# Where the operands of the dense matmuls begin in SBUF: multiples of 64 bytes in place of multiples of 16

## The chip, the cores and the metric

One core of a Trainium2 chip runs one program. The metric is the device time of one execution in microseconds. Three executions of the kernel before gave 1210.40, 1216.53 and 1216.72 us, a median of 1216.53 us.

## What is computed

Two blocks run one after the other on 256 tokens of width 1024, all in float32. The first is a Mamba-2 and RG-LRU hybrid with a gated feed-forward; the second has two layers, each with three mixers (retention, top-k attention, dilated attention) and an MLP of width 4096. Cut to the dense products, which are nearly all of the work:

```
proj = rmsnorm(x) @ w_in                        # 1024 -> 9760
h    = x + (g_ssm*(y_ssm @ w_out_ssm) + g_lru*(y_lru @ w_out_lru)) @ w_out
h    = h + (silu(gate) * up) @ w_ffn_out        # gate, up = split(rmsnorm(h) @ w_ffn_in), 1024 -> 2*2816
for layer in 0, 1:
    x = x + concat(retention, dsa, dilated)(rms_norm(x) @ w_in_2[layer]) @ w_out_2[layer]
    x = x + square(relu(rms_norm(x) @ w_up_2[layer])) @ w_down_2[layer]     # 1024 -> 4096 -> 1024
return rms_norm(x)
```

## The kernel before

Every dense product is done in a split form. A float32 operand is held as a pair of tiles, `hi` (rounded to the matmul's F32R format by ScalarE) and `lo` (the rest, by VectorE), and a product is three matmuls: hi by hi, hi by lo, lo by hi (`mm3`, L329, and L380 to L382).

The weights stream from HBM on the SP queue into three raw buffers (`emit_dma`, L222). `emit_split` (L240) turns a piece of 1024 columns into `hi` (L253, ScalarE) and `lo` (L254, VectorE), four pieces ahead of their use, in five buffers each of 4,096 bytes a partition. `run_a` (L334) uses a 128x128 slice of the weights as the stationary operand (loaded by a weight load ahead of each matmul) and 256 columns of activations as the moving one. `run_b` (L360) does it the other way round: 128 tokens of the activations are stationary, and up to 512 columns of weights move. Small side tasks (convolutions, scans, attention, norms) are cut into steps that `tick` (L285) puts between groups of the dense matmuls, in an order fixed when the program is built.

The activations that are dense operands lie in these tiles: `xn` (the normalised input of a stage, one pair of 8 x 256 columns, reused by six stages in turn; `xn_tiles`, L406, with offsets from `XOFF`, L56); `uh`, `ul`, `sTh`, `sTl`, `lTh`, `lTl` and `mx0`, `mx1` (parts of the first block's mixers, pool `p1`); `ah`, `al` (feed-forward, L980); `mxh`, `mxl` (mixers of the second block, L877); `mah`, `mal` (MLP of each layer, L1297). An element takes 4 bytes, a row of 256 columns 1,024 bytes, and the 128-wide weight slices are 512 bytes apart, so that within a stage all operands of one kind begin at the same place modulo 512.

The starts that the allocator gives, in bytes modulo 512, and the number of dense matmuls that the loops issue:

```
stage (activation tile)           matmuls            activations  weights  moving minus stationary
in (xn 1)                         1848 of 256 cols   288          288      0
lg, wl, ws, wo (uh, lT, sT, mx)   876 of 256         480          288      192
ffn in (xn 3)                     1056 of 256        256          288      480
ffn out (ah)                      528 of 256         448          288      160
mixers 0 (xn 5), run_a            384 of 256         384          288      96
mixers 0 (xn 5), run_b            144 of 512         384          288      416
mixer outputs (mxh 6, mxh 11)     192 of 256, twice  32           288      256
up 0 (xn 8)                       768 of 256         480          288      192
down 0 (mah 0)                    768 of 256         480          288      192
mixers 1 (xn 10), run_a           384 of 256         32           288      256
mixers 1 (xn 10), run_b           144 of 512         32           288      256
up 1 (xn 13)                      768 of 256         304          288      16
down 1 (mah 1), run_b             288 of 512, 192 of 256   448    288      352
```

Modulo 64 the weights begin at 32, and so do the activations at 288, 480 and 32; those at 256, 384 and 448 begin at 0, and those at 304 at 48. One unit of each mixer stage (`kw`, 72 columns) has slices at other places.

Of the kernel before, what the change touches and what calls it, by code (L numbers as in the profile page):

```python
# [10 lines left out]
F32 = mybir.dt.float32  # L11
F32R = mybir.dt.float32r
# [5 lines left out]
T = 256  # L18
# [33 lines left out]
FM, QM, UM = (2, 3), (0, 0), (2, 3)  # L52

XOFF = ((8, 24), (0, 16), (32, 48), (56, 72), (72, 88), (12, 28))  # L56


CT = {"ident": 0, "tri": 128, "dup": 512}
# [63 lines left out]
def _build(ctx, tc, nc, A, out):  # L123
    cp = ctx.enter_context(tc.tile_pool(name="cp", bufs=1))
# [191 lines left out]
    def tpb():  # L316
        return bank("tp", 1)
# [85 lines left out]
    xn_n = [0]  # L403
    xn_s = [0]

    def xn_tiles():  # L406

        offs = XOFF[xn_s[0]]
        xn_s[0] += 1
        xn_n[0] += 1  # L410
        ab = []
        for k, o in zip("hl", offs):
            t = cp.tile([128, 8 * T + 112], F32R, tag=f"xn{k}", name=f"xn{k}{xn_n[0]}")
            ab.append(t[:, o:o + 8 * T].rearrange("p (k t) -> p k t", t=T))
        return ab

    def opnd(pair):
        return lambda k: (pair[0][:, k, :], pair[1][:, k, :])
# [66 lines left out]
    def split_into(hi, lo, src):  # L485
        S.activation(hi, src, AF.Copy)
        V.tensor_sub(lo, src, hi.bitcast(F32))  # L487
# [3 lines left out]
    with ExitStack() as st0:  # L491
# [30 lines left out]
        xn = xn_tiles()  # L522
# [11 lines left out]
        for f in range(0, 8, 2):  # L534
            t = p0.tile([128, 2, T], F32, tag="nx", bufs=2, name=f"nx{f}")
# [9 lines left out]
    p1x = ExitStack()  # L545
    ac = p1x.enter_context(tc.tile_pool(name="ac", bufs=1, side="right", reuse_waits="tile"))
    acs = ac.tile([128, 8, T], F32, name="acs")
    acl = ac.tile([128, 8, T], F32, name="acl")
    p1c = ExitStack()
    p1 = p1c.enter_context(tc.tile_pool(name="p1", bufs=1, side="right", reuse_waits="tile"))  # L550
    X = opnd(xn)
# [192 lines left out]
    ut, hl, lo_t = {}, {}, {}  # L744
# [131 lines left out]

    def mix_tiles(pool):  # L877
        xn_n[0] += 1
        return (pool.tile([128, 8, T], F32R, name=f"mxh{xn_n[0]}"), pool.tile([128, 8, T], F32R, name=f"mxl{xn_n[0]}"))

    class Norm:

# [78 lines left out]
    def rbb(rb, n):  # L961
        return rb[:, None, :].to_broadcast([128, n, T])
# [14 lines left out]

    with ExitStack() as st:
        pf = st.enter_context(tc.tile_pool(name="pf", bufs=1, side="right", reuse_waits="tile"))
        ah = pf.tile([128, 22, T], F32R, name="ah")  # L980
        al = pf.tile([128, 22, T], F32R, name="al")
        X = opnd(nrm.xn)
        for i, (a, b) in enumerate(FT):
            bg = run_a(f"fg{i}", X, hook=nrm.hook(FM) if i == 0 else None)
            sg = []
            for c, ps in enumerate(bg):
                t = pf.tile([128, 2, T], F32, tag="sg", bufs=4, name=f"fsg{i}{c}")
                V.tensor_mul(t, ps.rearrange("p (a b) -> p a b", b=T), rbb(nrm.rb, 2))
                S.activation(t, t, AF.Silu)
                sg.append(t)  # L990
            bu = run_a(f"fu{i}", X)
            for c, ps in enumerate(bu):
                t = pf.tile([128, 2, T], F32, tag="su", bufs=2, name=f"fsu{i}{c}")
                V.tensor_mul(t, ps.rearrange("p (a b) -> p a b", b=T), rbb(nrm.rb, 2))
                V.tensor_mul(t, t, sg[c])
                k = a + 2 * c
                split_into(ah[:, k:k + 2, :], al[:, k:k + 2, :], t)
        wfa = pf.tile([128, 8], F32, name="wfa")
        V.tensor_mul(wfa, pv[:, PV["normf"]:PV["normf"] + 8], pv[:, PV["attn"]:PV["attn"] + 8])
        wfac = cp.tile([128, 8], F32, name="wfac")  # L1000
        V.tensor_copy(wfac, wfa)
        nrm = Norm(lambda t: wfac[:, t:t + 1], second=lambda t: pvc("normf", t))
        for n in range(2):
            banks = run_a(f"fo{n}", opnd((ah, al)))
            for i, ps in enumerate(banks):
                nrm.bank_done(ps, 4 * n + 2 * i)
# [287 lines left out]
    def mlp(l, nrm):  # L1294
        with ExitStack() as st:
            pf = st.enter_context(tc.tile_pool(name=f"pf{l}", bufs=1, side="right", reuse_waits="tile"))
            ah = pf.tile([128, 32, T], F32R, name=f"mah{l}")  # L1297
            al = pf.tile([128, 32, T], F32R, name=f"mal{l}")
            X = opnd(nrm.xn)
            last = l == 1  # L1300
            if last:
                xr = pf.tile([128, 2, D], F32, name="xr")
                fw = pf.tile([128, D], F32, name="fw")
                brow(fw, 608, 608 + D, nc.gpsimd)

                def resid_t():
                    for b in range(2):
                        for c in range(2):
                            ps = tpb()
                            for t in range(4):  # L1310
                                PE.transpose(ps[:, t * 128:t * 128 + 128], h[:, 4 * c + t, b * 128:b * 128 + 128], ident)
                            S.activation(xr[:, b, c * 512:c * 512 + 512], ps, AF.Copy)
                            yield from pause("resid_t1", 1)

            for i in range(8):
                bu = run_a(f"up{i}_{l}", X, hook=nrm.hook(UM) if i == 0 else None)
                if last and i == 0:
                    side.append(resid_t())
                for c, ps in enumerate(bu):
                    k = 4 * i + 2 * c  # L1320
                    t = pf.tile([128, 2, T], F32, tag="mt", bufs=2, name=f"mt{l}{i}{c}")
                    a = pf.tile([128, 2, T], F32, tag="ma", bufs=2, name=f"ma{l}{i}{c}")
                    V.scalar_tensor_tensor(t, ps.rearrange("p (a b) -> p a b", b=T), 0.0, rbb(nrm.rb, 2),
                                           op0=OP.max, op1=OP.mult)
                    S.activation(a, t, AF.Square)
                    split_into(ah[:, k:k + 2, :], al[:, k:k + 2, :], a)
            drain()
            if not last:
                nrm2 = Norm(lambda t: pvc("attn", 8 + t), act=True)
                for n in range(2):  # L1330
                    banks = run_a(f"dn{n}_{l}", opnd((ah, al)))
                    for i, ps in enumerate(banks):
                        nrm2.bank_done(ps, 4 * n + 2 * i)
                return nrm2
            ssf = pf.tile([128, 2, 3], F32, name="ssf")
            for n in range(2):
                if n:
                    warm = sm.tile([128, 1], F32, name="warm")
                    S.activation(warm, ssf[:, 1, 0:1], AF.Sqrt)
                banks = run_b(f"dn{n}_{l}", opnd((ah, al)), tail=3 if n else 1, halves=n == 1)  # L1340
                for b in range(2):
                    parts = ((0, 0, 512), (1, 0, 512)) if n == 0 else ((0, 0, 512), (1, 0, 256), (2, 256, 256))
                    parts = parts[b:1 + b * len(parts)]
                    for i, (k, c0, w) in enumerate(parts):
                        if n and i + 1 == len(parts):
                            part = sm.tile([128, 1], F32, tag="part", name=f"part{b}")
                            V.tensor_scalar(part, ssf[:, b, 0:1], 1.0 / D, EPS, op0=OP.mult, op1=OP.add)
                            if i:
                                V.scalar_tensor_tensor(part, ssf[:, b, 1:2], 1.0 / D, part, op0=OP.mult, op1=OP.add)
                        d = xr[:, b, 512 * n + c0:512 * n + c0 + w]  # L1350
                        V.tensor_add(d, d, banks[k][:, 0:w])
                        q = pf.tile([128, 512], F32, tag="fq", bufs=2, name=f"fq{n}{b}{i}")
                        S.activation(q[:, 0:w], d, AF.Square, accum_out=ssf[:, b, n + i:n + i + 1])
                    if n:
                        r = rsqrt_act(ssf[:, b, len(parts):len(parts) + 1], 1.0 / D, part, f"rf{b}")
                    if n == 0:
                        V.tensor_mul(xr[:, b, 0:512], xr[:, b, 0:512], fw[:, 0:512])
                    else:
                        d0, d1 = xr[:, b, 0:512], xr[:, b, 512:1024]
                        S.activation(d0, d0, AF.Identity, scale=r)  # L1360
                        nc.sync.dma_start(out[0, 128 * b:128 * b + 128, 0:512], d0)
                        V.scalar_tensor_tensor(d1, d1, r, fw[:, 512:1024], op0=OP.mult, op1=OP.mult)
                        nc.sync.dma_start(out[0, 128 * b:128 * b + 128, 512:1024], d1)
# [39 lines left out]
```

## Time and profile before

| | |
|---|---|
| median of three executions | 1216.53 us |
| the profiled execution, its own time | 1216.44 us |
| its span, from the first to the last instruction | 1214.7 us |
| matmuls busy | 1202.6 us, 99% |
| weight loads busy | 1133.3 us, 93% |
| VectorE busy | 846.8 us, 70% |
| ScalarE busy | 700.5 us, 58% |
| the costliest group of matmuls (L330 on `xn`) | 1736 of them, mean record 284 ns |

Matmuls are pipelined: the record of one lasts some 280 ns, and the next begins long before it ends. What counts is the distance from one start to the next, here called the spacing. A stretch of the trace that is full of matmuls gives it as its length over the number that begin in it.

### The profile page before, as it was taken

What the parts mean: (1) busy time and instruction counts of PE and PEld (TensorE: products, weight loads), DVE (VectorE), ACT (ScalarE), POOL (GpSimd) and SP (SyncE); (2) the same over time, 40 slices, a digit from 0 to 9 for tenths busy, and PEclk for the clock granted to TensorE, in tenths of its full rate; (3) what the DMA queues carried; (4) which work ended last, traced back from release to release, by engine and by line L of the source; (5) the groups of instructions that cost most, each with busy time, mean ns of one, the idle gap of its engine ahead of it and who ended that gap; (6) DMA issues with size and microseconds to landing.
All of it is one profiled execution on the core that took longest, in us unless ns stands there. A gap on an engine that the chain in (4) does not pass through costs nothing.

```text
span 1214.7 us, 22653 instructions
## 1 busy us (share of the span) xinstructions
PE 1202.6 (99%) x9369; PEld 1133.3 (93%) x9369; DVE 846.8 (70%) x1483; ACT 700.5 (58%) x1071; POOL 4.6 (0%) x12
## 2 busy tenths in 40 slices
PE   8999999999999999999999999999999999999997
PEld 8999999999999999999897899999997969999886
DVE  7888988987686666557967586655479586666453
ACT  7698788767466444444546575544355376655342
POOL 0000000000000000000000000000000000000000
PEclk9999999999999999999999999999999999999999
DMA  8455444656555655545353455555554434565550
GB/s 299 135 176 172 151 145 150 206 175 204 196 177 177 197 182 178 185 159 194 121 178 105 138 175 179 196 182 183 169 163 143 134 105 158 185 194 175 192 189 35
DMA packets 109382, 205.21 MB, mean 169 GB/s; under 512 B 5792, under 2 KB 15776, under 8 KB 109152
## 3 DMA queue, kind: packets, MB, share of 16 engines
q1 hardware_dynamic: 108560, 201.09, 50.9%
q0 software_dynamic: 576, 2.62, 0.6%
q8 instruction: 73, 1.20, 0.4%
q14 instruction: 29, 0.24, 0.1%
q10 hardware_dynamic: 144, 0.07, 0.0%
HBM read 202.71 MB, written 1.05 MB: 168 GB/s over the span
## 4 chain that ended last, share of the span: by engine, by line
PE 94%; DVE 4%; ACT 1%; DMA 0%; issue 0%; SPq 0%; ACTq 0%
PE ps_mm L330 25%; PE ps_mm L332 25%; PE ps_mm L331 25%; PE ps_mm L380 3%; PE ps_mm L382 3%; PE ps_mm L381 3%; PE ps_sc L327 2%; PE ps_o L1123 1%; PE ps_o L688 1%; DVE lo L254 1%; DVE acc L1069 1%; PE ps_tp L1110 1%; DVE m L1068 1%; PE ps_sc L669 1%; PE ps_tp L941 0%; DMA xt<-in_x 0%
## 5 line engine op out<-in xcount | busy, mean ns | idle before, releaser
L254 DVE TENSOR_TENSOR lo<-raw,hi 128x1024 fp32r<-128x1024 f32 (+2 forms) x382 | 461.9, 1213 | 284.5 <-ACT hi L253 281.4
L253 ACT ACTIVATE hi<-raw 128x1024 fp32r<-128x1024 f32 (+2 forms) x382 | 400.6, 1053 | 425.9 <-PE ps_mm L331 332.5
L330 PE MATMUL ps_mm<-xnh,hi 128*128 128x256 f32 x1736 | 492.4, 284 | 0.0
L331 PE MATMUL ps_mm<-xnl,hi 128*128 128x256 f32 x1736 | 490.3, 283 | 0.0
L332 PE MATMUL ps_mm<-xnh,lo 128*128 128x256 f32 (+1 forms) x1736 | 489.2, 282 | 0.0
L330 PEld LDWEIGHTS ps_mm<-xnh,hi 128*128 128x128 f32 x1736 | 327.9, 189 | 3.8 <-issue 2.5
L331 PEld LDWEIGHTS ps_mm<-xnl,hi 128*128 128x128 f32 x1736 | 329.2, 190 | 1.3 <-DVE xnl L487 0.2
L332 PEld LDWEIGHTS ps_mm<-xnh,lo 128*128 128x128 f32 (+1 forms) x1736 | 328.2, 189 | 0.4 <-issue 0.2
L330 PE MATMUL ps_mm<-mah,hi 128*128 128x256 f32 x256 | 71.9, 281 | 0.0
L331 PE MATMUL ps_mm<-mal,hi 128*128 128x256 f32 x256 | 71.9, 281 | 0.0
L332 PE MATMUL ps_mm<-mah,lo 128*128 128x256 f32 x256 | 71.9, 281 | 0.0
L382 PE MATMUL ps_mm<-hi,mal 128*128 128x256 f32 (+1 forms) x160 | 56.2, 351 | 0.0
L381 PE MATMUL ps_mm<-lo,mah 128*128 128x256 f32 (+1 forms) x160 | 55.9, 349 | 0.0
L380 PE MATMUL ps_mm<-hi,mah 128*128 128x256 f32 (+1 forms) x160 | 55.7, 348 | 0.0
L330 PE MATMUL ps_mm<-ah,hi 128*128 128x256 f32 x176 | 49.2, 280 | 0.0
L331 PE MATMUL ps_mm<-al,hi 128*128 128x256 f32 x176 | 49.2, 280 | 0.0
L332 PE MATMUL ps_mm<-ah,lo 128*128 128x256 f32 x176 | 49.2, 280 | 0.0
L331 PEld LDWEIGHTS ps_mm<-mal,hi 128*128 128x128 f32 x256 | 49.2, 192 | 0.0
L330 PEld LDWEIGHTS ps_mm<-mah,hi 128*128 128x128 f32 x256 | 48.1, 188 | 0.0
L332 PEld LDWEIGHTS ps_mm<-mah,lo 128*128 128x128 f32 x256 | 48.1, 188 | 0.0
L380 PE MATMUL ps_mm<-hi,xnh 128*128 128x512 f32 x96 | 39.1, 407 | 0.0
L382 PE MATMUL ps_mm<-hi,xnl 128*128 128x512 f32 x96 | 37.8, 394 | 0.0
(384 smaller groups left out, 1885.1 us busy)
## 6 DMA issues: line engine op xcount, KB each, us to landing
raw<-in_w_in SPq DMA_DIRECT2D x61, 1024.0 KB, 5.1
raw<-in_w_up SPq DMA_DIRECT2D x32, 1024.0 KB, 5.4
raw<-in_w_down SPq DMA_DIRECT2D x32, 1024.0 KB, 5.0
raw<-in_w_ffn_in SPq DMA_DIRECT2D x22, 1024.0 KB, 5.2
raw<-in_w_ffn_out SPq DMA_DIRECT2D x10, 1024.0 KB, 5.1
raw<-in_w_out_ssm SPq DMA_DIRECT2D x8, 1024.0 KB, 5.1
raw<-in_w_out SPq DMA_DIRECT2D x16, 512.0 KB, 3.8
raw<-in_w_out_lru SPq DMA_DIRECT2D x4, 1024.0 KB, 5.0
```

What stands on the lines that cost most here:

```text
L253: S.activation(hi, raw, AF.Copy)
L254: V.tensor_sub(lo, raw, hi.bitcast(F32))
L327: PE.matmul(o, w, x_, start=True, stop=True)
L330: PE.matmul(ps, wh, xh, start=start, stop=False, skip_group_check=True)
L331: PE.matmul(ps, wh, xl, start=False, stop=False, skip_group_check=True)
L332: PE.matmul(ps, wl, xh, start=False, stop=stop, skip_group_check=True)
L380: PE.matmul(o, xh[:, ts], hi[:, k, cs], start=st, stop=False, skip_group_check=True)
L381: PE.matmul(o, xh[:, ts], lo[:, k, cs], start=False, stop=False, skip_group_check=True)
L382: PE.matmul(o, xl[:, ts], hi[:, k, cs], start=False, stop=sp, skip_group_check=True)
L669: PE.matmul(o, idr[:, hh:hh + 1].to_broadcast([64, 128]), csp, start=(i == 0), stop=True, skip_group_check=True)
L688: PE.matmul(ps[64 * i:64 * i + 64, c], xtok[g][:, b, (2 * j + i) * 64:(2 * j + i) * 64 + 64], M[:, i, m], start=(j % 2 == 0 and b == 0), s ...
L1068: V.max(m8, acc[:, a:b])
```

## The change

`XOFF` goes; a table `OFF` holds the offset of each pair, in elements, for all dense stages, and a helper `pair_tiles` allocates a pair with some room to spare (128 elements for most, 112 and 104 for `xn`) and returns the view that begins at the offset. `ah`, `mah` and `mx` pairs are made by it too. The lower half of `xn` becomes 8 elements (32 bytes) narrower and `acl` 32 bytes wider.

```
+OFF = {"in": (48, 64), "ffn": (64, 80), "mix0": (16, 32), "up0": (48, 64), "mix1": (32, 48), "up1": (48, 64),
+       "ah": (0, 0), "mx": (8, 8), "mah0": (120, 120), "mah1": (16, 16)}
+STAGES = ("in", "ffn", "mix0", "up0", "mix1", "up1")
...
+    def pair_tiles(pool, k, stage, names, tags=(None, None), pads=(128, 128)):
+        ab = []
+        for n, t, pad, o in zip(names, tags, pads, OFF[stage]):
+            kw = dict(tag=t) if t else {}
+            tl = pool.tile([128, k * T + pad], F32R, name=n, **kw)
+            ab.append(tl[:, o:o + k * T].rearrange("p (k t) -> p k t", t=T))
+        return ab
...
-            t = cp.tile([128, 8 * T + 112], F32R, tag=f"xn{k}", name=f"xn{k}{xn_n[0]}")
-            ab.append(t[:, o:o + 8 * T].rearrange("p (k t) -> p k t", t=T))
+        return pair_tiles(cp, 8, stage, (f"xnh{xn_n[0]}", f"xnl{xn_n[0]}"), ("xnh", "xnl"), (112, 104))
...
-    acl = ac.tile([128, 8, T], F32, name="acl")
+    acl = ac.tile([128, 8 * T + 8], F32, name="acl")[:, 0:8 * T].rearrange("p (k t) -> p k t", t=T)
...
-        return (pool.tile([128, 8, T], F32R, name=f"mxh{xn_n[0]}"), pool.tile([128, 8, T], F32R, name=f"mxl{xn_n[0]}"))
+        return pair_tiles(pool, 8, "mx", (f"mxh{xn_n[0]}", f"mxl{xn_n[0]}"))
...
-        ah = pf.tile([128, 22, T], F32R, name="ah")
-        al = pf.tile([128, 22, T], F32R, name="al")
+        ah, al = pair_tiles(pf, 22, "ah", ("ah", "al"))
...
-            ah = pf.tile([128, 32, T], F32R, name=f"mah{l}")
-            al = pf.tile([128, 32, T], F32R, name=f"mal{l}")
+            ah, al = pair_tiles(pf, 32, f"mah{l}", (f"mah{l}", f"mal{l}"))
```

What lies behind `xn` in the left part of SBUF (the weight buffers among it) moves down by 32 bytes, because `xn`'s lower tile is narrower. The first block's right-hand pool `p1` moves down by 32 bytes, because `acl` is wider and the pools on that side grow downwards from a fixed end. The pools that hold `ah`, `mah` and `mx` grow by 1,024 bytes. Counted through, the starts modulo 512 become: weights 256; in 448, ffn in 0, mixers 0 320, up 0 448, mixers 1 384, up 1 448; `uh`, `lT`, `sT`, `mx0`, `mx1` 448; `ah` 448; `mxh` 64; `mah0` 448; `mah1` 0. All are multiples of 64. Moving minus stationary is then 192 for in, lg, wl, ws, wo, ffn out, up 0, down 0 and up 1; 256 for ffn in and down 1; 64 and, in `run_b`, 448 for mixers 0; 128 and 384 for mixers 1; 320 for the mixer outputs. No instruction is added, taken away or moved.

## Rows read from the trace of the kernel before

**Rows 1.** The page, parts 1, 2 (40 slices) and 4 (chain that ended last).

```profile
PE 1202.6 (99%) x9369; PEld 1133.3 (93%) x9369; DVE 846.8 (70%) x1483; ACT 700.5 (58%) x1071; POOL 4.6 (0%) x12
...
PEclk9999999999999999999999999999999999999999
...
PE 94%; DVE 4%; ACT 1%; DMA 0%; issue 0%; SPq 0%; ACTq 0%
PE ps_mm L330 25%; PE ps_mm L332 25%; PE ps_mm L331 25%; PE ps_mm L380 3%; PE ps_mm L382 3%; PE ps_mm L381 3%; PE ps_sc L327 2%; PE ps_o L1123 1%; PE ps_o L688 1%; DVE lo L254 1%; DVE acc L1069 1%; PE ps_tp L1110 1%; DVE m L1068 1%; PE ps_sc L669 1%; PE ps_tp L941 0%; DMA xt<-in_x 0%
```

**Rows 2.** Waits of PE, longest: us in total, times, longest.

```profile
PE ps_tp L476 <- DVE yn L469: 1.6, 1, 1.6
PE ps_tp L476 <- DVE ync L441: 1.2, 2, 0.9
```

**Rows 3.** Windows of PE: stretch, length, busy (matmul records in it), clock, DMA share, GB/s.

```profile
14.00:39.00 25.00, 25.00 (x211) 1.00 0.73 245
70.00:90.00 20.00, 20.00 (x169) 1.00 0.48 151
...
212.00:222.00 10.00, 10.00 (x91) 1.00 0.71 216
...
348.00:369.00 21.00, 21.00 (x188) 1.00 0.62 198
385.00:495.00 110.00, 110.00 (x932) 1.00 0.57 182
497.00:557.00 60.00, 60.00 (x514) 1.00 0.55 182
625.00:640.00 15.00, 15.00 (x127) 1.00 0.23 72
686.00:699.00 13.00, 13.00 (x111) 1.00 0.56 178
701.00:708.00 7.00, 7.00 (x64) 1.00 0.42 141
714.00:791.00 77.00, 77.00 (x656) 1.00 0.56 186
792.00:881.00 89.00, 89.00 (x758) 1.00 0.56 181
...
1048.00:1116.00 68.00, 68.00 (x575) 1.00 0.59 186
```

**Rows 4.** Groups by line of PE in 700.3 to 708 us: busy, mean ns.

```profile
L330 PE MATMUL ps_mm<-xnh,hi 128*128 128x256 f32 x23 | 6.3, 276 | 0.0
```

**Rows 5.** Groups by line of PE in 713 to 791 us.

```profile
L330 PE MATMUL ps_mm<-xnh,hi 128*128 128x256 f32 x222 | 62.5, 281 | 0.0
```

**Rows 6.** Groups by line and shape of PE in 919 to 932 us (mixers 1).

```profile
L382 PE MATMUL ps_mm<-hi,xnl 128*128 128x512 f32 x18 | 7.0, 389 | 0.0
```

**Rows 7.** Windows of PE in down 1, where 512 columns move.

```profile
1119.00:1159.00 40.00, 40.00 (x173) 1.00 0.56 190
```

**Rows 8.** Timeline of PE, 707.9 to 709.8 us: start, length.

```profile
708.07 0.28 PE L332 MATMUL ps_mm<-xnh,lo 128*128 128x256 f32 x1
708.34 1.05 PE L941 MATMUL ps_tp<-ones,sqa 128*128 128x1 f32 x8
```

**Rows 9.** Windows of all engines: length, then busy of PE, PEld, DVE, ACT, POOL.

```profile
12.00:40.00 28.00, 28.00 (x233) 27.62 (x232) 26.40 (x42) 20.52 (x29) 0.00 (x0) 1.00 0.75 253
...
120.00:160.00 40.00, 40.00 (x331) 37.53 (x329) 37.49 (x73) 32.73 (x60) 0.00 (x0) 1.00 0.45 146
...
382.00:495.00 113.00, 113.00 (x957) 113.00 (x957) 73.87 (x81) 54.80 (x63) 0.00 (x0) 1.00 0.58 186
...
587.00:612.00 25.00, 24.79 (x116) 19.42 (x115) 24.65 (x87) 12.83 (x18) 0.00 (x0) 1.00 0.40 127
...
912.00:935.00 23.00, 22.06 (x104) 17.74 (x104) 22.71 (x84) 11.43 (x15) 0.00 (x0) 1.00 0.38 129
```

More of the change, by code (lines that the diff above doesn't have):

```diff
@@ L52 @@
 FM, QM, UM = (2, 3), (0, 0), (2, 3)
-XOFF = ((8, 24), (0, 16), (32, 48), (56, 72), (72, 88), (12, 28))
+OFF = {"in": (48, 64), "ffn": (64, 80), "mix0": (16, 32), "up0": (48, 64), "mix1": (32, 48), "up1": (48, 64),
+       "ah": (0, 0), "mx": (8, 8), "mah0": (120, 120), "mah1": (16, 16)}
+STAGES = ("in", "ffn", "mix0", "up0", "mix1", "up1")
 CT = {"ident": 0, "tri": 128, "dup": 512}
@@ L404, in _build @@
     xn_s = [0]
+    def pair_tiles(pool, k, stage, names, tags=(None, None), pads=(128, 128)):
[5 more added lines that the diff above has]
+        return ab
     def xn_tiles():
-        offs = XOFF[xn_s[0]]
+        xn_n[0] += 1
+        stage = STAGES[xn_s[0]]
         xn_s[0] += 1
-        xn_n[0] += 1
-        ab = []
-        for k, o in zip("hl", offs):
-            t = cp.tile([128, 8 * T + 112], F32R, tag=f"xn{k}", name=f"xn{k}{xn_n[0]}")
-            ab.append(t[:, o:o + 8 * T].rearrange("p (k t) -> p k t", t=T))
-        return ab
+        return pair_tiles(cp, 8, stage, (f"xnh{xn_n[0]}", f"xnl{xn_n[0]}"), ("xnh", "xnl"), (112, 104))
     def opnd(pair):
```

## The prediction

> **What bounds the kernel now.** I read the page first. Matmuls are busy for 99% of the span, the chain that ended last is TensorE for 94%, and most of that chain lies on the three lines of `mm3` [rows 1]. The list of waits says that this is no chain of stalls: the longest wait of TensorE for anything is 1.6 us [rows 2]. So the time is the number of matmuls times their spacing. The clock is not what varies, for the granted clock is full in every slice [rows 1] and 1.00 in every stretch [rows 3].
>
> The view that matters is therefore the table of steady stretches, one for each stage [rows 3]. A record of some 280 ns spans about 2.4 spacings, so a stretch holds 2.4 more records than matmuls begin in it, and the spacing is its length over (records - 2.4). That gives, for one and the same form (128x128 stationary, 256 columns moving):
>
> - in: 25.00 / 208.6 = 119.8 ns, and 20.00 / 166.6 = 120.0 ns later on;
> - `sT` and `wo` stretches: 10.00 / 88.6 = 112.9 and 21.00 / 185.6 = 113.1 ns;
> - ffn in: 110.00 / 929.6 = 118.3; ffn out: 60.00 / 511.6 = 117.3;
> - mixers 0: 15.00 / 124.6 = 120.4; mixer outputs: 13.00 / 108.6 = 119.7;
> - up 0: first 7.00 / 61.6 = 113.6, then 77.00 / 653.6 = 117.8; down 0: 89.00 / 755.6 = 117.8;
> - up 1: 68.00 / 572.6 = 118.8.
>
> The reader is to see levels: about 113.3, 117.8 and 120. The level goes with where the operands begin. Both stretches at 113 have 192 between moving and stationary starts; the stretches at distance 0 and 256 stand at 120; those whose two operands differ by 32 modulo 64 lie between and at 120. And it is not the start alone: up 0 runs at distance 192 throughout, yet its records last 276 ns until 708 us [rows 4] and 281 ns after 713 us [rows 5]. Between them the norm's eight one-column matmuls stand in the stream [rows 8]. A record lasts 163 ns longer than the spacing at every level, so 276 is 113 and 281 is 118. At distance 192 there are thus two rhythms, and an interruption can throw the stream from one into the other; it then stayed there for 170 us.
>
> **The change part by part.** No instruction, DMA, wait or queue position is added or moved. The helper and the table cost nothing on the chip; the padding takes room only. The tiles that move by 32 or 1,024 bytes keep their order, and the last readers of what lies under them are the same last matmuls of a stage, so I cost the moved buffers at nothing. If a reuse wait did appear it would show as a wait of ScalarE or VectorE, which are idle for 42% and 30% of the span [rows 1], and I bound it at 1 us on either side. What is left is the spacing of each stage, against the profiled execution's own 1216.4 us (0.1 us under the median).
>
> Stages brought to distance 192, taken at 113.3 ns:
> - in: 1848 x (119.9 - 113.3) = 12.2 us. Here the cover is thin: VectorE is busy 26.40 of 28 us and 37.49 of 40 us [rows 9], and a 5% shorter stretch would leave it no idle time. I take three quarters, 9.2 us.
> - ffn out: 528 x 4.0 = 2.1 us. It follows a stage at a 120 rhythm without interruption, as `wo` and the start of up 0 did, which fell into 113.
> - up 0: 696 x 4.5 = 3.1 us (its first 72 have it now); down 0: 768 x 4.5 = 3.4 us; up 1: 768 x 5.4 = 4.1 us. VectorE is at two thirds in such stages [rows 9], so nothing else comes late.
> - lg, wl, ws, wo: at 113 already, at the same distance: 0.
>
> Sum: 21.9 us.
>
> Stages at distance 256: ffn in goes from 118.3 to the 120 measured at 256 in the mixer outputs, 1056 x 1.7 = 1.8 us lost. Down 1 has 288 matmuls of 512 columns at 40.00 us / (173 - 1.7) = 233.5 ns [rows 7]; the same form at distance 256 has records of 389 ns in mixers 1 [rows 6], less 163 is 226, so 288 x 7 = 2.0 us are won; its 192 of 256 columns lose 0.2. Together 0.
>
> Stages at 64, 320, 128, 384 and 448: no row has these distances with both starts alike modulo 64. The nearest rows bound a 256-column matmul by 113.3 and 120.4 [rows 3], and one of 512 by 226 [rows 6] and twice 120. Mixers and mixer outputs are 1152 matmuls near 120, so between 7.7 us won and 0.5 lost. Of the 288 of 512 columns half (mixers 1) have 226 now and can lose 144 x 14 = 2.0; the other half, taken as 233 like down 1, can win or lose 1.0. I take 0, nearest to what they have; the mixers' middle is held by VectorE anyway, busy 24.65 of 25 and 22.71 of 23 us [rows 9].
>
> Sum of all: 21.9 + 0 = 22 us off 1216.4, which is **1194.5 us**.
>
> How much lower could a spacing go? The eight one-column matmuls take 1.05 us with a last record of 0.25 [rows 8], so 0.80 / 7 = 114 ns for weight load after weight load with nothing to stream; records at 113 show that it can be a little less. I take 111 as the floor of a 256-column stage. Below it no start can bring it; from 113.3 that is 2.3 x 7956 = 18 us at the very most.
>
> One rule of the Trainium skill speaks against the whole change. "TensorE: Matmul & The Clock Gate", in "Step-by-step: what each phase is for", says that the array reads SBUF through two independent ports, so that loading the next weights takes no bandwidth from the running matmul. By it the distance of the two operands can't matter, and the sum is 0. Stretches that differ in their starts alone differ by 6 ns a matmul [rows 3], which speaks against it here; but up 0 with two rhythms at one pair of starts [rows 4, 5] leaves it a chance, given below as the fourth rival.
>
> **The rivals.**
>
> 1. The slow rhythm at 192 stays. Up 0 after its norm, down 0 and up 1 take 117.8 although their distance is 192, because the interruption is the same one at the same place. For: rows 5 are just that. Against: `sT` and `wo` keep 113 among interruptions of other kinds, and the phase in which the stream resumes may differ with starts at 0 modulo 64. Then up 0 and down 0 give 0 and up 1 768 x 1.0 = 0.8: 22 - 3.1 - 3.4 - 3.3 = 12.2 us, **1204 us**.
>
> 2. The 64-byte boundary itself is what counts. 256 columns at one a cycle of 2.4 GHz would be 106.7 ns; 113.3 is 17/16 of that and 120 is 18/16, as if 256 columns that begin in the middle of a 64-byte line took one line more. With both operands on the boundary a clash would cost no more than 113.3 whatever the distance. For: the step between the levels is always 1/16 of 106.7. Against: ffn in and ffn out have moving operands on the boundary and are at 117 to 118 [rows 3]. Then ffn in wins 5.3 instead of losing 1.8, mixers and mixer outputs win some 4 (half of them held by VectorE or by attention), the rest of down 1 another 1 and its 512-column matmuls 2 more: 22 + 14 = 36 us, **1180 us**, and 1172 if half the way to the floor comes too.
>
> 3. Slower. Starting at 32 modulo 64 is part of what makes 192 fast, and on the boundary the streams lock at 120, the level of distances 0 and 256. The place is every stage that now lies below 120, first `lg`, `wl`, `ws` and `wo`: 876 x 6.7 = 5.9; ffn in 1.8, ffn out 1.4, up 0 and down 0 1464 x 2.2 + 72 x 6.7 = 3.7, up 1 0.9, down 1 1.9 at twice 120. That is 15.6 us, **1232 us**. It decides as soon as `sT` stretches leave 113. For: every stage with a moving operand on the boundary is above 117 now. Against: those all have weights off it.
>
> 4. The starts do nothing; the levels come from what else runs beside the stages. For: the two rhythms at one pair of starts. Against: level and start go together over ten stages and two halves of the program. **1216 us**.
>
> **How the numbers follow.** I give the forecast 0.32, rival 1 0.25, rival 2 0.22, rival 3 0.12, rival 4 0.09. The likeliest single case is the forecast, 1194.5 us. The range runs from 1173, which takes in most of rival 2, to 1217, which takes in rival 4; left out are rival 3 (0.12) and the lower edge of rival 2 (0.05). Within 0.5% means 1210.4 to 1222.6 us, about what a measurement of this kernel can tell from no change. Faster: the forecast, rival 2, and rival 1 but for 0.04 in which VectorE's cover in the first stage eats more, so 0.75. Slower: rival 3, 0.12. The same: the rest, 0.13.
>
> **What would show it.** In the table of stretches: in, ffn out, up 0, down 0 and up 1 with records of 276 ns; ffn in with 283; down 1 with 389 for 512 columns. Records of 281 from 713 us on mean rival 1, 276 in ffn in and the mixers rival 2, 283 in `sT` and `wo` rival 3, unchanged records everywhere rival 4. VectorE's idle time in the first 300 us should nearly vanish, and TensorE's waits there grow by no more than 3 us. The forecast is wrong if stages at distance 192 do not share one spacing, or if the first stage's VectorE gives back more than a quarter of what the spacing wins.

## The result, and the profile after

The changed kernel takes 1198.3 us (median of 4 runs, 1197.72 to 1200.14), the kernel before 1216.47 us in the same comparison (1210.4 to 1216.72): a ratio of 0.9859 with an interval of 0.9836 to 0.9882. The profiled execution took 1198.39 us, its span is 1196.6, so it stands for the median. The forecast was 1194.5 us, in a range of 1173 to 1217. The sign and most of the size were right; 3.8 us of the forecast gain did not come.

The page, parts 1, 2 and 4, of the kernel after, as in [rows 1]:

```profile
PE 1183.8 (99%) x9369; PEld 1115.4 (93%) x9369; DVE 844.9 (71%) x1483; ACT 700.4 (59%) x1071; POOL 4.6 (0%) x12
...
PEclk9999999999999999999999999999999999999999
...
PE 88%; DVE 6%; ACT 4%; issue 1%; DMA 0%; SPq 0%; ACTq 0%; DVEq 0%
```

Still 9369 matmul records, still 99% busy, still the full clock. The time in which matmuls are busy is 18.8 us shorter. On the chain VectorE has gone from 4% to 6% and ScalarE from 1% to 4%. All of that lies in the first stage: of the chain's first 347 us ScalarE now holds 45 us and VectorE 25, where they held 12 and 6.5. In some places of that stage TensorE now ends up behind them.

Windows of TensorE after (stretch, length, busy with the records in it, granted clock, DMA share, GB/s), to be held against [rows 3]. They are, in order, three from the first stage, the first output projection, ffn in, ffn out, mixers 0, their output, up 0 ahead of and behind the norm, down 0, up 1 and down 1:

```profile
14.00:38.00 24.00, 24.00 (x214) 1.00 0.78 263
...
70.00:86.00 16.00, 15.99 (x140) 1.00 0.39 125
...
171.00:184.00 13.00, 13.00 (x112) 1.00 0.42 125
...
345.00:364.00 19.00, 19.00 (x163) 1.00 0.60 195
380.00:490.00 110.00, 110.00 (x919) 1.00 0.56 181
495.00:552.00 57.00, 57.00 (x506) 1.00 0.56 185
620.00:635.00 15.00, 15.00 (x135) 1.00 0.25 79
680.00:692.00 12.00, 12.00 (x104) 1.00 0.58 192
695.00:702.00 7.00, 7.00 (x62) 1.00 0.40 140
708.00:782.00 74.00, 74.00 (x655) 1.00 0.60 193
784.00:869.00 85.00, 85.00 (x753) 1.00 0.57 190
...
1036.00:1100.00 64.00, 64.00 (x567) 1.00 0.61 198
1103.00:1143.00 40.00, 40.00 (x178) 1.00 0.59 202
```

Length over (records - 2.4), as in the prediction, gives the spacing. Ffn in: 110 / 916.6 = 120.0 ns (118.3 before). Ffn out: 57 / 503.6 = 113.2 (117.3). Behind the norm of up 0: 74 / 652.6 = 113.4 (117.8); down 0: 85 / 750.6 = 113.2 (117.8); up 1: 64 / 564.6 = 113.4 (118.8). Down 1 with 512 columns: 40 / (178 - 1.7) = 226.9 (233.5). In the first stage the reader is to see two levels and not one: 24 / 211.6 = 113.4 at the start, 13 / 109.6 = 118.6 at 171 us, and a mixture of both, 116.3, from 70 to 86. And the first output projection, which stood at 113.1 before, is at 19 / 160.6 = 118.3.

The two levels meet in up 0 again. Groups by line of TensorE after (busy, mean ns): from 694.3 to 702 us, from 708 to 782 us, then ffn in from 380 to 490 us and the 512 columns of down 1 from 1103 to 1143 us, the answers to [rows 4] and [rows 5] and two levels forecast from [rows 3, 6]:

```profile
L333 PE MATMUL ps_mm<-xnh,lo 128*128 128x256 f32 x23 | 6.5, 281 | 0.0
...
L332 PE MATMUL ps_mm<-xnl,hi 128*128 128x256 f32 x219 | 60.4, 276 | 0.0
...
L332 PE MATMUL ps_mm<-xnl,hi 128*128 128x256 f32 x307 | 86.9, 283 | 0.0
...
L383 PE MATMUL ps_mm<-hi,mal 128*128 128x512 f32 x60 | 23.3, 389 | 0.0
```

Up 0 is slow ahead of its norm (a spacing of 7 / 59.6 = 117.4) and fast behind it. Before, it was the other way round, 276 and then 281 [rows 4, 5], at the same distance of 192. The place of the switch is the same too, as the timeline of TensorE after shows (start, length):

```profile
702.34 0.28 PE L333 MATMUL ps_mm<-xnh,lo 128*128 128x256 f32 x1
702.46 0.95 PE L946 MATMUL ps_tp<-ones,sqa 128*128 128x1 f32 x8
703.27 0.36 PE L331 MATMUL ps_mm<-xnh,hi 128*128 128x256 f32 x1
```

In [rows 8] these eight one-column records end the fast rhythm; here they end the slow one. (The program issues four such matmuls; each leaves two records.) VectorE's cover, as in [rows 9] (busy of PE, PEld, DVE, ACT, POOL), after:

```profile
12.00:39.00 27.00, 26.77 (x233) 26.35 (x233) 26.28 (x43) 20.55 (x29) 0.00 (x0) 1.00 0.79 264
118.00:157.00 39.00, 39.00 (x329) 36.31 (x328) 37.28 (x74) 31.86 (x60) 0.00 (x0) 1.00 0.46 149
```

28 us have become 27 with 0.23 us in which TensorE has nothing to do, and VectorE is busy for 97% of it: the cover is used up there.

**Where the 18 us came from.** Summed from the starts of all matmul records of both traces, stage by stage (a minus is time won):

| stage | forecast, us | measured, us |
|---|---|---|
| in | -9.2 | -5.7 |
| lg, wl, ws, wo | 0 | +1.9 |
| ffn in | +1.8 | +1.7 |
| ffn out | -2.1 | -2.1 |
| mixers and their outputs | 0 | -2.4 |
| up 0 | -3.1 | -3.0 |
| down 0 | -3.4 | -3.4 |
| up 1 | -4.1 | -3.4 |
| down 1 | -1.8 | -1.7 |
| sum (of the unrounded rows) | -21.9 | -18.0 |

The sum and the difference of the spans (18.1) differ by what lies outside the stages.

### The profile page after: what moved, and what is told of

Read it like the earlier page. It is cut to its first block, busy times and chain, and to the rows that moved or that the text cites. A ratio compares the mean times of both kernels' runs of the same rounds, so it can differ in the third digit from the quotient of the medians.

```text
span 1196.6 us, 22653 instructions
## 1 busy us (share of the span) xinstructions
PE 1183.8 (99%) x9369; PEld 1115.4 (93%) x9369; DVE 844.9 (71%) x1483; ACT 700.4 (59%) x1071; POOL 4.6 (0%) x12
## 4 chain that ended last, share of the span: by engine, by line
PE 88%; DVE 6%; ACT 4%; issue 1%; DMA 0%; SPq 0%; ACTq 0%; DVEq 0%
PE ps_mm L331 24%; PE ps_mm L333 23%; PE ps_mm L332 23%; PE ps_mm L381 3%; PE ps_mm L383 3%; PE ps_mm L382 3%; PE ps_sc L328 2%; DVE lo L255 2%; PE ps_o L1127 1%; PE ps_o L693 1%; ACT hi L254 1%; DVE acc L1073 1%; PE ps_tp L1114 1%; DVE m L1072 1%; PE ps_sc L674 1%
```

## The experiments

From here on "fast" and "slow" are the rhythms of 113.3 and 117.8 ns; "distance" is moving start less stationary start, modulo 512. Single runs of the kernel before fall in two groups, near 1210.3 us (5 of 17 runs in the comparison of e1 to e4, 17 of 21 in that of e5 to e8, 3 of 11 in that of e9 to e11, 6 of 11 in that of e12; each comparison ran on a chip of its own) and near 1216.7; the medians of before below differ for that reason, and times are better compared than ratios.

### The same distances, all operands at 32 modulo 64 (e1_twin32)

```
-OFF = {"in": (48, 64), "ffn": (64, 80), "mix0": (16, 32), "up0": (48, 64), ...
+OFF = {"in": (56, 72), "ffn": (72, 88), "mix0": (24, 40), "up0": (56, 72), ...
```

(and so for every entry: 8 elements more, modulo 128. `acl` and the lower half of `xn` get their old widths back, which moves the weights by the same 32 bytes.)

> The changed kernel with every dense operand, stationary and moving, 32 bytes further on: all distances as after the change, but all starts at 32 modulo 64 and none on a 64-byte boundary. Distance theory (the spacing hangs on moving minus stationary start modulo 512 and not on the boundary): the same levels stage by stage, 120 ns in ffn in, 226 to 227 for 512 columns in down 1, 113 or 118 at distance 192, and 1198 us, between 1194 and 1203 because the two rhythms at 192 may fall otherwise. Boundary theory (the gain comes from starting on 64 bytes): most of the 18 us is lost, 1208 to 1216 us.

Measured: 1202.28 us (1198.72 to 1206.85, 6 runs), ratio 0.9893 [0.9865, 0.9922]. Windows of TensorE, ffn in and up 0 behind its norm:

```profile
380.00:485.00 105.00, 105.00 (x878) 1.00 0.56 182
...
708.00:778.00 70.00, 70.00 (x620) 1.00 0.58 192
```

105 / 875.6 = 119.9 and 70 / 617.6 = 113.3: the levels of the changed kernel, 32 bytes off every boundary. The multiple of 64 is not what counts; the distance is. The 4 us between the medians are not a level of their own: three runs lie at 1198.7 to 1199.7 us, as the changed kernel does, and three at 1204.9 to 1206.9, 6.5 us later in the mean, about what up 0 and down 0 cost in the other rhythm (next experiment). The profile is of the first group; that the second is those two stages is not shown.

### Ffn in at 192 too (e2_ffn192)

```
-"ffn": (64, 80)
+"ffn": (48, 64)
```

> The changed kernel with ffn in at distance 192 in place of 256. Distance theory: its 1056 matmuls leave 120 ns for 113.3 (7.0 us won, 1191 us) or for the slow rhythm 117.8 (2.3 us won, 1196 us). Rival, that the level of a stage comes from what runs beside it: ffn in stays at 120 and the time at 1198 us.

Measured: 1192.9 us (1191.25 to 1198.58, 6 runs), ratio 0.9818 [0.979, 0.9845]. Windows of TensorE: ffn in, up 0 behind its norm, down 0:

```profile
380.00:485.00 105.00, 105.00 (x929) 1.00 0.60 193
...
708.00:778.00 70.00, 70.00 (x597) 1.00 0.57 193
784.00:860.00 76.00, 76.00 (x647) 1.00 0.53 172
```

Ffn in is at 105 / 926.6 = 113.3. But this profiled execution is one of the two near 1198.6, and it shows why: up 0 and down 0 are at 117.7 and 117.9. They have the starts that they have in the changed kernel, where they ran at 113.3. The four other runs lie at 1191.3 to 1192.9, in the mean 6.5 us below these two; (696 + 768) x 4.4 = 6.4 us accounts for that.

### Mixers 1 at 64 as well (e3_ffn192_mix1_64)

```
-"mix1": (32, 48)
+"mix1": (16, 32)
```

> The changed kernel with ffn in at 192 and the mixers of layer 1 at 64, as those of layer 0 are. Distance theory: beside what ffn in wins, the 384 matmuls of 256 columns in mixers 1 leave 118.7 for 113.3 to 117.8 and win 0.3 to 2 us, those of 512 columns stay near 233: 1189 to 1196 us. Rival (what runs beside it): 1198 us.

Measured: 1191.98 us (1189.99 to 1196.89, 5 runs), ratio 0.981 [0.9784, 0.9837]. In the profiled run (1189.99) mixers 1 have a mean of 115.1 ns where the changed kernel has 118.6, and up 0 and down 0 are fast:

```profile
708.00:778.00 70.00, 70.00 (x620) 1.00 0.60 196
784.00:860.00 76.00, 76.00 (x673) 1.00 0.56 187
```

Between the profile of this run and the last one lie 8.6 us, and only about 1.2 of them are the edit, as the theory had it for these stages. The medians of the two kernels, 0.9 us apart, do not show it by themselves.

### The kernel before, with the first stage alone at 192 (e4_before_in192)

```
-XOFF = ((8, 24), (0, 16), ...
+XOFF = ((56, 72), (0, 16), ...
```

> The kernel before with one part of the change alone: the first stage (in) at distance 192, starts at 480 and 288, so at 32 modulo 64; everything else as before. Distance theory: its 1848 matmuls leave 120 for a mix of 113.3 and 117.8, 4 to 9 us won, 1207 to 1213 us. Boundary theory: nothing is on a 64-byte boundary, so nothing is won, 1216 us.

Measured: 1212.57 us (1205.84 to 1213.82, 12 runs) against 1216.67, ratio 0.997 [0.9951, 0.9989]. Windows of TensorE: the first stage at 14 and 68 us, the output projection, up 0 behind its norm:

```profile
14.00:38.00 24.00, 24.00 (x214) 1.00 0.79 257
...
68.00:87.00 19.00, 19.00 (x164) 1.00 0.44 136
345.00:364.00 19.00, 19.00 (x164) 1.00 0.60 195
...
708.00:778.00 70.00, 70.00 (x620) 1.00 0.61 197
```

This gives 4.1 us for the largest term of the forecast and the loss beside it together; the changed kernel's two rows, -5.7 and +1.9, make 3.8. Summed in the same way, this trace has -5.9 and +1.9. It shows both halves. The first stage starts fast (113.4) and is slow by 68 us (19 / 161.6 = 117.6). And the projection, whose operands nobody moved, goes from 113.1 [rows 3] to 117.6: the stage before it now has the same distance and hands its slow rhythm on, where before, at distance 0, it had none to hand on. The last row is the other half of the lottery: up 0, with the very starts that it has in the kernel before, at 70 / 617.6 = 113.3, in one of two runs near 1205.9; ten lie at 1211.7 to 1213.8. So the fast rhythm is to be had there without the change, in some executions.

### All stages at 64, at 448, at 320 (e5_all64, e6_all448, e7_all320)

```
-OFF = {"in": (48, 64), "ffn": (64, 80), ... "ah": (0, 0), "mx": (8, 8), "mah0": (120, 120), ...
+OFF = {"in": (16, 32), "ffn": (16, 32), ... "ah": (96, 96), "mx": (72, 72), "mah0": (88, 88), ...
```

(this is 64; for 448 and 320 the pairs are (112, 0) and (80, 96), with ah, mx and mah0 at 64, 40, 56 and at 32, 8, 24. In all three down 1 stays at 256, and lg, wl, ws, wo with the first output projection at 192.)

> The changed kernel with every dense stage but down 1 at a distance of 64 modulo 512 (in, ffn in, ffn out, both mixers with their mixed tiles, up 0, down 0, up 1). Theory (the distance sets a pair of rhythms, 113.3 and 117.8 ns, at every odd multiple of 64, and each long stretch of matmuls falls into one of them when it starts): stretches in both rhythms, none at 118.3 or 120 in these stages, single runs spread over 4 us or more, median 1188 to 1198 us. Rival (64 has only the fast rhythm, as mixers 0 showed at this distance): every stretch at 113.3 ns, the runs within 1 us of each other, near 1185 us.

> The same stages at a distance of 448 modulo 512, a distance that no stretch of 256-column matmuls has had so far. Theory (two rhythms at any odd multiple of 64): as at 64, 113.3 and 117.8 ns mixed, median 1188 to 1198 us. Rival (the level falls or rises steadily with the distance up to 512, where it is 120): 118.3 to 120 ns everywhere, as at 480 and at 0, so 1210 us or more.

> The same stages at a distance of 320 modulo 512, which only the mixed tiles of the mixers had before, at 117.8 ns in every long stretch. Theory (two rhythms at any odd multiple of 64): 113.3 and 117.8 ns mixed, median 1188 to 1198 us. Rival (320 has the slow rhythm alone): all of these stages at 117.8 ns, the runs within 1 us of each other, about 1198.4 - 2.3 (ffn in) - 0.4 (mixers 1) + 2.3 (ffn out) + 3.8 (in) + 1.1 (mixers 0) + 3.0 (up 0) + 3.4 (down 0) + 3.2 (up 1) = 1212 us.

Measured: 64 gives 1209.12 us (1208.77 to 1209.69, 11 runs), 320 gives 1209.42 (1208.69 to 1209.73, 11 runs), 448 gives 1195.44 (1188.59 to 1196.46, 5 runs), beside 1210.34 for the kernel before; ratios 0.9982 [0.9969, 0.9995], 0.9984 [0.9971, 0.9997] and 0.9852 [0.9826, 0.9878]. Windows of TensorE at 64: start and end of the first stage, the first output projection, ffn in, up 0:

```profile
14.00:38.00 24.00, 24.00 (x207) 1.00 0.76 259
...
322.00:342.00 20.00, 20.00 (x172) 1.00 0.58 189
346.00:363.00 17.00, 17.00 (x153) 1.00 0.57 184
383.00:485.00 102.00, 102.00 (x868) 1.00 0.57 186
...
711.00:771.00 60.00, 60.00 (x512) 1.00 0.55 177
```

At 320, the first and the last of these:

```profile
14.00:38.00 24.00, 24.00 (x206) 1.00 0.77 262
...
711.00:771.00 60.00, 60.00 (x512) 1.00 0.55 180
```

And at 448, all five:

```profile
14.00:38.00 24.00, 24.00 (x214) 1.00 0.78 262
...
322.00:342.00 20.00, 20.00 (x172) 1.00 0.54 194
346.00:363.00 17.00, 17.00 (x147) 1.00 0.53 169
383.00:485.00 102.00, 102.00 (x902) 1.00 0.60 197
...
711.00:771.00 60.00, 60.00 (x512) 1.00 0.59 192
```

64 and 320 stand at 117.3 to 117.9 in each stage that was moved. 448 is at 113.4 at the start and in ffn in, and slow at the end of the first stage and in up 0. For 64 both theory and rival missed: it has both rhythms, but of some 6,800 matmuls at 64 only some 420 ran fast, all in short stretches, and at 320 only some 270; at 448 it was some 4,100, at 192 in the changed kernel some 4,000 of 5,470. So 64 and 320 fall into the slow rhythm and stay, and their runs lie within 1.1 us of each other; 192 and 448 have both, more often the fast one, and scatter. For 320 the rival was right in the main (1209.4 us for its 1212), for 448 the theory. The pattern repeats after 256 bytes in these four.

The output projection has a distance of 192 in all three kernels, and the stage ahead of it ends slow in each (20 / 169.6 = 117.9 at 64 and 448). Behind 64 it still starts fast, 17 / 150.6 = 112.9, and behind 320 too; behind 448 it stays slow, 17 / 144.6 = 117.6. So at this border a slow stretch ran on where the two distances are equal or 256 apart, and not where they differ otherwise.

Mixers 0 at 64, which gave the hope of a fast 64, had been luck: in this run of the kernel at 64 the same stretch of 154 matmuls is slow.

### Small matmuls in down 0 (e8_poke)

```
+def poke():
+    ...
+    for i in range(1 + n % 3):
+        PE.matmul(ps[:, i:i + 1], nrm.acc[0][:, 0, 0:128], ones[:, 0:1], ...)
```

> The changed kernel with small matmuls of one column (their results aren't used) put into down 0 after every fourth pair of tiles: one, two, three, one, two, three of them and so on. Down 0 otherwise runs 768 matmuls without a break at one spacing, 113.3 ns in the profile of the changed kernel. Theory (the rhythm is settled when a stretch starts and then held): the stretches between the small matmuls are each at 113.3 or at 117.8 ns from their first to their last matmul, and at least one change of level falls on a break. Rival (the rhythm belongs to the stage and its data, not to the start): all stretches at the same level, and the breaks only add their own 0.2 to 0.5 us each.

Measured in one execution: 1205.53 us. Groups by line of TensorE from 789.6 to 876 us:

```profile
L333 PE MATMUL ps_mm<-mal,hi 128*128 128x256 f32 x234 | 64.7, 276 | 0.0
L1342 PE MATMUL ps_tp<-ones,sqa 128*128 128x1 f32 x60 | 7.5, 229 | 0.0
```

There are fifteen breaks (the later expectations count fourteen), and each small matmul leaves two records. Each stretch behind one holds one level, as the theory says, but it is the same in all, 113.3; the change of level that it wanted did not come. The rival holds for this execution: the breaks only cost their 0.5 us each (down 0 takes 94.1 us and not 87.0).

### Breaks at which TensorE waits (e11_poke_wait)

```
+PE.matmul(ps[:, 0:w], nrm.acc[0][:, 0, 0:128], ident[:, 0:w], ...)
+S.activation(t[:, 0:w], ps[:, 0:w], AF.Copy)
+PE.matmul(ps[:, 256:257], ident, t[:, 0:1], ...)
```

> As e8_poke, but TensorE waits at each of the fourteen breaks of down 0: a small matmul, a copy of its result by ScalarE (1, 64 or 128 columns in turn), and a one-column matmul on the copy; results not used. Theory (it is the wait that makes the start of a stretch fall on either rhythm, as behind the norm's matmuls, which wait for ScalarE or VectorE): of the fourteen stretches behind the breaks some at 113.3 and some at 117.8 ns. Rival (at a distance of 192 down 0 always starts at 113.3 ns and is slow only where up 0 hands the slow rhythm on): all fourteen at 113.3 ns.

Measured in one execution: 1208.29 us. Groups by line of TensorE behind two neighbouring breaks, 834.3 to 838 us and 839.3 to 844 us:

```profile
L334 PE MATMUL ps_mm<-mah,lo 128*128 128x256 f32 x11 | 3.1, 281 | 0.0
...
L334 PE MATMUL ps_mm<-mah,lo 128*128 128x256 f32 x14 | 3.9, 276 | 0.0
```

Thirteen of fifteen came out fast, two slow. So a break in the middle of one stage, at one pair of starts, can leave either rhythm, which the rival excludes. That it is the wait that does it is not settled by this: the two stretches at 117.8 ns are also those before which 15 and 8 matmuls, not 3 or 4, stand between the two small matmuls. The wait is short: the second small matmul starts 121 to 247 ns behind the matmul ahead of it. At both breaks that left 117.8 ns it was 227 ns; of the thirteen that left 113.3 ns, five had less and eight more.

### The 448 kernel again, and with three restarts (e10_all448_again, e9_448_restart)

```
+def poke(delay):
+    ...
+    for i in range(2):
+        PE.matmul(ps[:, i:i + 1], ident, ones[:, 0:1], ...)
```

(ahead of the output projection, and a few microseconds behind the norms of ffn in and up 0.)

> The kernel of e6_all448 once more, beside e9_448_restart on the same chip. Theory (the rhythm is chosen afresh in every execution): again runs in two groups near 1188.8 and 1195.6 us, and a profile in which some of the long stretches have the other rhythm than in the profile of e6_all448. Rival (the rhythm belongs to the program): the same stretches at the same spacing as there, and one group of runs.

> All stages at 448 modulo 512 as in e6_all448, and one pair of one-column matmuls (results not used) put in at three places, so that the long stretches start anew without a wait: ahead of the first output projection of stage 1, soon after the norm's matmuls of ffn in, and soon after those of up 0. In e8_poke all fourteen stretches behind such matmuls ran at 113.3 ns, and the stretch from 300 to 374 us and that of up 0 and down 0 ran at 117.8 ns in the profile of e6_all448. Theory (a stretch that has fallen into the slow rhythm keeps it until it is interrupted, and an interruption without a wait starts the fast one): the projection, ffn in, ffn out, up 0 and down 0 at 113.3 ns behind the added matmuls, the group of runs near 1195.5 us gone, all runs between 1186 and 1190 us. Rival (the added matmuls choose as blindly as the norm's do): both groups stay, 1188 to 1197 us, about 0.5 us longer for each pair.

Measured: the same program again took 1189.62 us (1188.36 to 1191.41, 6 runs), ratio 0.9794 [0.9767, 0.982]; with the restarts 1202.89 us (1202.61 to 1203.71, 6 runs), ratio 0.9903 [0.9879, 0.9926]. Windows of TensorE of the first, up 0 and down 0:

```profile
711.00:771.00 60.00, 60.00 (x532) 1.00 0.59 192
790.00:860.00 70.00, 70.00 (x620) 1.00 0.55 182
```

512 records of the same program in 60 us have become 532: the rhythm is not a property of the program. The second group near 1195.6 did not show in these six runs, which were on another chip; the five of e6_all448, on one chip, had both, two near 1188.8 and three near 1195.8. With the restarts, ffn in, the same stretch of up 0, and down 0:

```profile
383.00:485.00 102.00, 102.00 (x869) 1.00 0.58 186
...
711.00:771.00 60.00, 60.00 (x512) 1.00 0.57 182
790.00:860.00 70.00, 70.00 (x597) 1.00 0.54 171
```

Half of the theory held: the runs lie within 1.1 us, where the same kernel without the added matmuls reached over 3.1 and 7.9 us. The half that mattered fell: every stretch behind an added matmul is slow. The rival fell as well, by 6 us. In ffn in the records last 276 to 277 ns up to the small matmuls at 381.6 us and 281 ns behind them.

### The restart with another operand (e12_448_restart_ones)

```
-PE.matmul(ps[:, i:i + 1], ident, ones[:, 0:1], ...)
+PE.matmul(ps[:, i:i + 1], ones, ones[:, 0:1], ...)
```

> e9_448_restart with one operand changed: the added small matmuls take their stationary operand from the tile of ones (it begins 224 bytes into a block of 512, as the accumulator did in e8_poke) and not from the identity (352 bytes into it). In e8_poke all fourteen stretches behind such matmuls were at 113.3 ns; in e9_448_restart all three places were followed by 117.8 ns. Theory (the small matmul's own operands set the phase at which the stretch starts, and with it the rhythm): the stretches behind the three places at 113.3 ns, so against 1202.9 us about 264 x 4.4 ns = 1.2 us less in the first, 1500 x 4.4 ns = 6.7 us in ffn in and out, 1404 x 4.4 ns = 6.2 us in up 0 and down 0: near 1189 us, and all runs within 2 us of each other. Rival (the place or the distance of 448 decides, and the accumulator's start had no part in it): again 1203 us. Second rival (chance): runs spread between 1189 and 1203 us.

Measured: 1190.37 us (1189.02 to 1191.27, 6 runs), ratio 0.9811 [0.9783, 0.9839]. The same three windows:

```profile
383.00:485.00 102.00, 102.00 (x903) 1.00 0.58 194
...
711.00:771.00 60.00, 60.00 (x532) 1.00 0.59 194
790.00:860.00 70.00, 70.00 (x620) 1.00 0.56 186
```

113.3 ns in all three, and the output projection as well (17 / (153 - 2.4) = 112.9). One operand of six small matmuls, two at each place, of which no result is used, is worth 12.5 us. The two kernels ran on different chips; what ties the difference to the operand is that in each profile all the stretches behind the added matmuls have one and the same rhythm. The theory's 1189 and its spread of 2 us held nearly (2.25 us). Only the two tiles with starts of 352 and 224 were tried, so that it is the start of that operand, and not something else in which the tiles differ, is not shown. Nor is it a rule for every distance: in e11_poke_wait, at 192, the identity was the stationary operand of the last small matmul of each break, and thirteen of fifteen stretches behind it were fast.

## Why the prediction was right, and where it was short

**The distance, not the boundary, sets the levels: right.** Ffn in at 256 went to 120.0, ffn out at 192 to 113.2, 512 columns at 256 to 226.9, each within 0.3 us of its term. The same moving start, 448, gave ffn out 117.3 with weights at 288 and 113.2 with weights at 256. The kernel with everything at 32 modulo 64 has the same levels, which ends rival 2; ffn out, up 1 and down 0 below 114 on the boundary end rival 3. Its sign did come in part, as the projection and some of the `sT` stretches left 113; but they went to 118 and not to 120, and the projection does the same off the boundary (117.6 in e4_before_in192). Rival 2 also rested on a misreading: the step between the levels is not always 1/16 of 106.7, 6.7 ns; from 113.3 to 117.8 it is 4.5. Rival 4 falls by ffn in alone, 113.3, 117.8 and 120.0 ns at 192, 64 and 256 with the same work beside it. The rule of the Trainium skill that the prediction weighed ("TensorE: Matmul & The Clock Gate", "Step-by-step: what each phase is for": loading weights takes no bandwidth from the running matmul) would have given no change. These runs do not fit it for this mix of loads and moving operands; what the two operands share is not shown.

**The first stage: the mis-sized term.** 12.2 us gross less a quarter for VectorE, 9.2, was forecast; 5.7 came. The quarter was about right: breaks and waits grew by 2.3 us, most of it in places where VectorE or ScalarE now comes late. VectorE's idle time in the first 300 us did not nearly vanish, as the prediction had it; it went from 47.7 to 44.0 us, and the cover is thin only in spots. The rest was taken at one spacing, 113.3, and came out at a mean of 115.4, because the stage fell into the slow rhythm in part: some 1,780 x 2.1 = 3.7 us. The prediction had named two rhythms at 192, and then priced this stage at one of them. It also wrote that the forecast is wrong if stages at distance 192 do not share one spacing. They do not: the projection has 118.3, ffn out 113.2, and the first stage both. The time came near the forecast all the same, because most of the matmuls at 192 ran fast.

**lg, wl, ws, wo: a cost left out.** Costed at nothing because the distance does not change (both starts move by 32 bytes); 1.9 us were lost. Before, their neighbours had distance 0 and they began anew; now the neighbours have 192 too, and a slow stretch runs on into them. Moving the first stage alone in the kernel before reproduced it, +1.9 us, and the kernels at 64 and 320, where the projection starts fast behind a slow stretch, are the counter-test.

**Up 0 and down 0: the right number, at least in part by luck.** 6.5 us were forecast as stages "brought to distance 192", and 6.4 came in this profile. But they had 192 before. With the starts of the kernel before they run at 113.3 in some executions (the profile of e4_before_in192), and on the boundary at 117.8 in others (that of e2_ffn192). So the change is not needed for this gain and does not ensure it: rival 1, at 0.25, described for these two stages what happens in a share of the executions on either side of the change. Whether the change shifts that share is open. In the comparison of e1 to e4 the faster group has 5 of 17 runs of the kernel before and 2 of 12 of e4_before_in192, but 4 of 6 of e2_ffn192 and 4 of 5 of e3_ffn192_mix1_64, which have the changed kernel's starts in these stages (e1_twin32: 3 of 6). That leans towards a part of the change, by few runs. If it has one, it need not be the stages' own starts: the norm's accumulator, the stationary operand of its one-column matmuls, moves with them, by the allocation from 256 to 224 modulo 512. Measured against the group of before near 1210.3 us, the change is worth 12 us, not 18.

**Mixers: nothing was forecast, 2.4 us came**, within the bounds given (7.7 won to 0.5 lost, before the 512 columns): 64 ran partly fast, 320 at 118.1. **Up 1** gave 3.4 for 4.1, because in the mean over all its matmuls it had stood at 118.4 and not 118.8, and its breaks grew by 0.4.

Open: what fixes the rhythm at a break. Small matmuls without a wait fixed it the same way at each of their places, one tile fast and another slow; behind the norm's it differs between executions of one program. The weights began at 256 or 288 in every run, so the distance was varied nearly by the moving operand's start alone.

## What to carry to other kernels

When a stage is matmul after matmul with a new stationary operand each, compare the spacing between stages that differ only in where the operands begin: here a distance of 192 or 448 between moving and stationary starts made 113.3 ns possible, 64 and 320 settled at 117.8, and 0 and 256 stood at 120 (while 512 columns did best at 256). Where one distance shows two spacings, don't price a stage at the better one; take several profiles, and compare times by group before giving an edit the credit. A version that beats both kernels is the one at 448: 1189.6 and 1195.4 us in two comparisons without the restarts, 1190.4 with those on the tile of ones, against 1198.3 in the first comparison.

## What was not expected of the hardware

- One program has two execution times 6.4 us apart (1210.3 and 1216.7), with the granted clock at 0.997 to 0.999 in both, near the price of 1,464 matmuls at 113.3 or at 117.8 ns (6.6 us). The profile of e4_before_in192 shows these stages in the fast rhythm; the kernel before itself was profiled in the slower group only.
- Two one-column matmuls whose results are not used set the spacing of the 924 + 528 matmuls behind them, 113.3 ns with the tile of ones as their stationary operand and 117.8 with the identity. With such a pair at three places the kernel at 448 takes 1190.4 or 1202.9 us.
- 512 columns: 226.9 ns at a distance of 256 (down 1), and in the mixers some 229 at 64, 232 at 384 and 233 at 192 and 448, all with both starts on multiples of 64.
